# State-space and selection stages of a hybrid encoder step, rewritten on the vector engine: GELU without GpSimd, early weight remainders on DVE, a shorter threshold update and five-pass marks

## Chip, cores and metric

One core of one Trainium2 chip runs the kernel. The time is the device time of one execution in microseconds (us). Engines are named as in the profile: PE (TensorE), DVE (VectorE), ACT (ScalarE), POOL (GpSimd), SP (issues transfers).

## What is computed

One inference step of one layer, for 1024 prompt tokens and 32 sample tokens with 1024 channels:

```python
h = rms_norm(x, g_norm) * (1 + scale) + shift
z = h @ w_in                       # u, zs, q, k, v, za, qi, ki, wi, gates
hr, hi = scan(ab * h + bb @ u)     # S5: 32 groups, 64 complex states each
ys = gelu(c_re @ hr - c_im @ hi + d_skip * u)
ys = ys * sigmoid(ys @ w_glu + b_glu) * silu(zs)
score = sum_h(wi * relu(qi . ki))  # indexer; top 256 (sample: 136) keys
ya = softmax(q . k[selected]) @ v[selected] * silu(za)
out = (sigmoid(g_s) * (ys @ w_ps) + sigmoid(g_a) * (ya @ w_pa)) @ w_o
y = rms_norm(x + gate * out, g_final)
```

It also returns the keys, values, indexer keys and final states. All inputs and outputs are float32.

## The kernel before

**Precision.** A product of float32 matrices is made from three PE passes. Each weight tile is loaded raw, rounded to a high part (wh, by ACT, L46), and the remainder wl = raw - wh is taken by POOL (L49); PE then does wh x hH, wh x hL and wl x hH (L220 to L222). `ztile` (L626) does this for one tile of 128 output columns: 3 groups of tokens times 8 steps of depth times 3, so 72 matmuls of 128x352. Buffers for raw, wh and wl are two deep, so wh of tile n + 2 waits until PE has done tile n.

**Stages, in time.** From 0 to 66 us modulation, RMSNorm and the transposition of h, in an order written out by hand; DVE's state-space constants are held in a list and let go a few at a time. From 66 to about 112 us DVE works on the rest of these constants, while PE does u tiles and the first gate tiles. The constants include the powers TCt and TSt (128 of them for each of 16 state columns), doubled in seven steps (L415), each of which ends in `renorm`, six tiny DVE operations that bring the last power back to length 1.

From 110 to 250 us the state-space model runs in four quarters q = 0 to 3 of 8 groups. `build(q)` (L682) makes the matrices ER, EI (L698 to L700, DVE, each from two products in e2), G2 (L708 to L710), the skip term dm (L727) and the kernel Ksb (L734); PE transposes ER and EI (L723) and multiplies them. `chain_in` sends u through PE, `chain_scan` (L765) does rotation, scan and rotation back on DVE and leaves HS, `chain_out` (L803) multiplies with Tq (L811) and G2 (L812), copies the result to Yq (ACT, L813) and applies GELU on half quarters: Square on ACT (L817), two POOL operations (L818, L819), Tanh on ACT (L820), and one DVE operation (L821). Yq has one buffer; it is stored to DRAM as yD[q] when both halves are done. PE fills in with u and gate tiles. For q = 0 the G2 part of `build` runs on DVE, for the others on POOL.

GLU follows (257 to 315 us), which loads yD back, then the indexer's scores (315 to 445 us).

From 445 to 659 us come the selection and projections. The k-th largest score of each row is found bit by bit in 32 steps (`Grp.step`, L1162): in each, every row counts its scores at or above a trial threshold, on DVE for three score tiles (group A), on ACT for four (groups B1 and B2), and two or three tiny DVE operations set the bit. `mark` (L1194) then turns the threshold into a mask mb for each of the seven tiles: 1 for scores above it and for as many of the equal ones as are still needed, counted by a scan, as an addend of 0 or -BIG. PE meanwhile does the q, k, v and gate projections. The attention heads (L1052 scores into PSUM, L1053 adds the mask on DVE) begin when the masks stand.

Outside the part written by hand the order is set by the scheduler of the tile framework, which lays out each engine's instructions by a simulated timeline; each engine then takes its instructions strictly in that order.

Of the kernel before, what the change touches and what calls it, by code (L numbers as in the profile page):

```python
# [18 lines left out]
G3 = 352  # L19
KT = 8  # L20
EPS = 1e-6
BIG = 1e30
NCH = 133
NST = 134
QT = [(i * 128, 128, 128 * (i + 1)) for i in range(8)]
# [9 lines left out]
def body(nc, tc, I, O, dbg=None):  # L35
# [180 lines left out]
    def wsplit(src, kt, n, pool=None, heng=None, leng=None):  # L216
        return wparts(wload(src, kt, n, pool), kt, n, pool, heng, leng)
# [197 lines left out]
    for k in range(7):  # L415
        n = 1 << k
        cmul(TCt[:, :, n + 1:2 * n + 1], TSt[:, :, n + 1:2 * n + 1], TCt[:, :, 1:n + 1], TSt[:, :, 1:n + 1],
             bc(col(TCt, n), n), bc(col(TSt, n), n), n)
        renorm(2 * n)
    for t in (TCt, TSt):  # L420
        ve.tensor_copy(t[:, :, 129:134], t[:, :, 0:5])
    rho = tp_.tile([128, 16, 1], F32)
# [198 lines left out]
    stA.close()  # L621
    stQ.close()

    hz = [se]

    def ztile(c0, ncol, evac):  # L626
        wh, wl = wsplit(w_in[:, c0:c0 + ncol], KT, ncol, heng=hz[0])
        for n in range(3):
            ps = ps_z("pz")
            for k in range(KT):  # L630
                mm3(ps[:ncol, :G3], wh[:, k], wl[:, k], hH[n][:, k], hL[n][:, k], k == 0, k == KT - 1)
            evac(n, ps[:ncol, :G3])
# [49 lines left out]
    def build(q):  # L682
        Uq = xq.tile([128, 8, NCH], F32, name="Uq", bufs=2)
        sp.dma_start(Uq, uD[q].rearrange("(g m) s c -> (m s) g c", m=16))
        pr = slice(4 * q, 4 * q + 4)
        ER, EI = (xq.tile([128, 4, 16, 8], F32, name=n) for n in ("ER", "EI"))
        G2 = xq.tile([128, 8, 16, 8], F32, name="G2", bufs=2)
        e4 = [128, 4, 16, 8]

        def pw(t, lo):  # L690
            return t[:, pr, lo:lo + 8].unsqueeze(2).to_broadcast(e4)

        def bm(t):
            return t[:, pr].unsqueeze(3).to_broadcast(e4)

        def lin(eng, out, a, b, c, d, op):
            e2 = xq.tile(e4, F32, name="e2", tag="e2" + ("v" if eng is ve else "g"))
            eng.tensor_tensor(out, a, b, op=ALU.mult)  # L698
            eng.tensor_tensor(e2, c, d, op=ALU.mult)
            eng.tensor_tensor(out, out, e2, op=op)  # L700

        lin(ve, ER, pw(RR, 0), bm(BR), pw(RI, 0), bm(BI), ALU.subtract)
        lin(ve, EI, pw(RR, 0), bm(BI), pw(RI, 0), bm(BR), ALU.add)
        eng = ve if q == 0 else ge
        for e in range(2):
# [24 lines left out]
        for k in range(4):  # L730
            o = pt[:, 32 * k:32 * k + 32]
            te.matmul(o, fl(ER, k), CD[0][:, k], start=True, stop=False)
            te.matmul(o, fl(EI, k), CD[1][:, k], start=False, stop=True)
        ve.tensor_tensor(Ksb.rearrange("p g m -> p (g m)"), pt[:, 0:128], dm.rearrange("p g m -> p (g m)"), op=ALU.add)  # L734
        Tq = xq.tile([128, 8, 16, 8], F32, name="Tq", bufs=2)
        for hb in range(2):
            pT = ps_t()
            for s4 in range(4):
                te.matmul(pT[:, 128 * s4:128 * (s4 + 1)], shm[:, 4 * hb + s4], Ksb.rearrange("p g m -> p (g m)"),
                          start=True, stop=True)  # L740
            v = pT.rearrange("p (s g m) -> p g m s", s=4, m=16)
# [61 lines left out]
    def chain_out(q, ops, HS):  # L803
        Uq, G2, Bc, Tq = ops
        Yq = xq.tile([128, 8, NCH], F32, name="Yq")
        for g in range(8):
            k, r = g // 2, slice(64 * (g % 2), 64 * (g % 2) + 64)
            if g % 2 == 0:
                py = ps_s("py")
            o = py[:, 512 * (g % 2):512 * (g % 2) + NCH]  # L810
            te.matmul(o, Tq[:, g].rearrange("p m s -> p (m s)"), Uq[:, g], start=True, stop=False)  # L811
            te.matmul(o, G2[:, g].rearrange("p m s -> p (m s)"), HS[:, g % 2, g // 2, 0:NCH], start=False, stop=True)  # L812
            se.copy(Yq[:, g], o)  # L813
            if g % 4 == 3:
                yh = Yq[:, g - 3:g + 1]
                a1 = xq.tile([128, 4, NCH], F32, name="a1")
                se.activation(a1, yh, AF.Square)  # L817
                ge.tensor_scalar(a1, a1, 0.044715, 1.0, op0=ALU.mult, op1=ALU.add)  # L818
                ge.tensor_mul(a1, a1, yh)  # L819
                se.activation(a1, a1, AF.Tanh, scale=math.sqrt(2.0 / math.pi))  # L820
                ve.scalar_tensor_tensor(yh, a1, 1.0, yh, op0=ALU.add, op1=ALU.mult)  # L821
        sp.dma_start(yD[q].rearrange("(g m) s c -> (m s) g c", m=16), Yq)
# [322 lines left out]
    class Grp:  # L1145
# [16 lines left out]
        def step(self, b):  # L1162
# [11 lines left out]
                                 op0=ALU.bitwise_xor)  # L1174
                return
            x = self.thr
            if b or self.sign:
                ve.tensor_scalar(self.nxt, x, (1 << b - 1) if b else -(1 << 31), None, op0=ALU.bitwise_xor)
                x = self.nxt
            if self.sign:  # L1180
                ve.tensor_tensor(self.keep, self.cnt, self.lim, op=ALU.is_ge)  # L1181
            else:
                ve.tensor_tensor(self.keep, self.cnt, self.nse, op=ALU.is_lt)
            ve.scalar_tensor_tensor(self.thr, self.keep, b, x, op0=ALU.logical_shift_left, op1=ALU.bitwise_xor)

    A, B1, B2 = Grp(GA, "a", False), Grp(GB[:2], "b", True), Grp(GB[2:], "c", True)
    junk = sel.tile([128, 1024], BF16, tag="j", bufs=3, name="junk")
# [6 lines left out]
    def mark(g):  # L1194
        for k, m, nk, x in g.tiles():
            tk = g.thr.bitcast(F32)[:m, k:k + 1]
            cum = sel.tile([128, 1024], F32, name="cum")
            gt, eq = (sel.tile([128, 1024], BF16, name=n, tag="j", bufs=3) for n in ("gt", "eq"))
            ve.tensor_scalar(gt[:m, :nk], x[:m], tk, None, op0=ALU.is_gt, op1=ALU.add, accum_out=g.cnt[:m, k:k + 1])
            need = sel.tile([128, 1], F32, name="need", bufs=2)  # L1200
            ve.tensor_sub(need[:m], g.nse[:m, k:k + 1], g.cnt[:m, k:k + 1])
            ve.tensor_scalar(eq[:m, :nk], x[:m], tk, None, op0=ALU.is_equal)
            ve.tensor_tensor_scan(cum[:m, :nk], eq[:m, :nk], eq[:m, :nk], 0.0, op0=ALU.add, op1=ALU.max)
            ve.scalar_tensor_tensor(eq[:m, :nk], cum[:m, :nk], need[:m], eq[:m, :nk], op0=ALU.is_le, op1=ALU.mult)
            ve.tensor_tensor(gt[:m, :nk], gt[:m, :nk], eq[:m, :nk], op=ALU.max)
# [226 lines left out]
```

## Time and profile before

| | |
|---|---|
| median of 3 runs | 1135.89 us (1133.39 to 1137.15) |
| profiled execution | 1129.1 us, span 1127.3 us |
| mean granted PE clock | 0.961 |
| PE busy | 1026.3 us (91%), 6122 matmuls |
| DVE busy | 815.2 us (72%), 1922 instructions |
| ACT busy | 538.4 us (48%), 1129 instructions |
| POOL busy | 310.7 us (28%), 323 instructions |
| chain that ended last | PE 53%, DVE 28%, ACT 5%, issue 4%, DMA 3%, POOL 1% |

Busy shares are averages over stages with different limits. The chain follows the last instruction back to what released it; its shares tell on which engine the end was waiting, not how busy that engine was. In a waiting row, what stands behind the arrow is the instruction whose end released the waiting one.

### The profile page before, as it was taken

What the parts mean: (1) busy time and instruction counts of PE and PEld (TensorE: products, weight loads), DVE (VectorE), ACT (ScalarE), POOL (GpSimd) and SP (SyncE); (2) the same over time, 40 slices, a digit from 0 to 9 for tenths busy, and PEclk for the clock granted to TensorE, in tenths of its full rate; (3) what the DMA queues carried; (4) which work ended last, traced back from release to release, by engine and by line L of the source; (5) the groups of instructions that cost most, each with busy time, mean ns of one, the idle gap of its engine ahead of it and who ended that gap; (6) DMA issues with size and microseconds to landing.
All of it is one profiled execution on the core that took longest, in us unless ns stands there. A gap on an engine that the chain in (4) does not pass through costs nothing.

```text
span 1127.3 us, 17022 instructions
## 1 busy us (share of the span) xinstructions
PE 1026.3 (91%) x6122; PEld 943.5 (84%) x6122; DVE 815.2 (72%) x1922; ACT 538.4 (48%) x1129; POOL 310.7 (28%) x323
## 2 busy tenths in 40 slices
PE   6899898998999999978999969899996899999996
PEld 2689798998998899977899959789895699998774
DVE  5889999843435655999999975967748966687433
ACT  3541243435235545786786224655656665334111
POOL 2212535535030011232232202323227611220000
PEclk9989998999999999989999979999897999999998
DMA  9724213227331012231223322222333332854311
GB/s 357 191 76 116 76 39 78 77 89 230 124 98 47 19 57 89 84 90 53 76 96 96 124 59 57 66 87 57 95 91 110 114 113 86 232 167 144 126 62 51
DMA packets 115656, 115.50 MB, mean 102 GB/s; under 512 B 13372, under 2 KB 92688, under 8 KB 115572
## 3 DMA queue, kind: packets, MB, share of 16 engines
q1 hardware_dynamic: 115336, 114.36, 33.4%
q8 instruction: 48, 0.79, 0.3%
q14 instruction: 36, 0.29, 0.1%
q0 software_dynamic: 160, 0.03, 0.0%
q10 hardware_dynamic: 76, 0.02, 0.0%
HBM read 79.55 MB, written 30.08 MB: 97 GB/s over the span
## 4 chain that ended last, share of the span: by engine, by line
PE 53%; DVE 28%; ACT 5%; issue 4%; DMA 3%; POOL 1%; SPq 0%; DVEq 0%; POOLq 0%; ACTq 0%
PE pz L220 9%; PE pz L221 8%; PE pz L222 8%; DVE junk L1168 4%; PE pss L1052 3%; PE psm L1401 3%; PE psm L1403 3%; PE psm L1402 3%; PE pt L1108 2%; ACT junkb L1166 2%; PE pspo L1118 2%; PE pspo L1117 1%; PE pss L947 1%; PE pss L948 1%; PE psm L220 1%
## 5 line engine op out<-in xcount | busy, mean ns | idle before, releaser
L220 PE MATMUL pz<-hH,wh 128*128 128x352 f32 (+1 forms) x1080 | 361.7, 335 | 17.8 <-DVE zt L645 9.4
L221 PE MATMUL pz<-hL,wh 128*128 128x352 f32 (+1 forms) x1080 | 358.3, 332 | 0.7
L222 PE MATMUL pz<-hH,wl 128*128 128x352 f32 (+1 forms) x1080 | 356.9, 330 | 0.0
L49 POOL TENSOR_TENSOR wl<-raw,wh 128x1024 fp32r<-128x1024 f32 (+1 forms) x68 | 149.6, 2201 | 308.8 <-ACT wh L46 251.7
L220 PEld LDWEIGHTS pz<-hH,wh 128*128 128x128 f32 (+1 forms) x1080 | 208.2, 193 | 24.2 <-DVE zt L645 10.5
L221 PEld LDWEIGHTS pz<-hL,wh 128*128 128x128 f32 (+1 forms) x1080 | 207.8, 192 | 4.6 <-DVE hL L49 2.2
L222 PEld LDWEIGHTS pz<-hH,wl 128*128 128x128 f32 (+1 forms) x1080 | 207.6, 192 | 1.2
L1168 DVE TENSOR_SCALAR_CACHE_REDUCE junk<-sco,thra 128x1024 bf16<-128x1024 f32 (+2 forms) x96 | 96.8, 1009 | 0.3
L955 DVE SCALAR_TENSOR_TENSOR sco<-rl,wi,sco 128x384 f32<-128x384 f32 (+6 forms) x49 | 49.5, 1016 | 35.1 <-ACT rl L950 33.8
L46 ACT CAST wh<-raw 128x1024 fp32r<-128x1024 f32 (+2 forms) x53 | 46.5, 880 | 56.2 <-PE pz L221 36.6
L1053 DVE CUSTOM_DVE_ANT_0 Sm<-pss,mb 128x512 f32<-128x512 f32 (+4 forms) x68 | 39.8, 592 | 46.1 <-PE pt L1108 42.6
L1056 ACT ACTIVATE Sm<-Sm,mx 128x128 f32<-128x128 f32 (+8 forms) x68 | 52.9, 778 | 34.1 <-DVE mx L1053 33.6
L1110 ACT CAST PH<-pt 128x512 fp32r<-128x512 f32 (+2 forms) x96 | 44.4, 480 | 51.6 <-PE pspo L1117 26.1
L1166 ACT ACTIVATE junkb<-sco,thrb 128x896 bf16<-128x896 f32 x64 | 59.9, 936 | 17.9 <-DVE keepc L1181 6.4
L950 ACT ACTIVATE rl<-pss 128x384 f32<-128x384 f32 (+6 forms) x56 | 40.7, 737 | 48.8 <-PE pss L948 44.3
L1111 DVE TENSOR_TENSOR PL<-pt,PH 128x512 fp32r<-128x512 f32 (+2 forms) x96 | 51.5, 550 | 7.7 <-ACT PH L1110 5.9
L1403 PE MATMUL psm<-o,mL 128*128 128x512 f32 (+1 forms) x144 | 56.7, 395 | 0.0
L1401 PE MATMUL psm<-o,mH 128*128 128x512 f32 (+1 forms) x144 | 56.5, 394 | 0.0
L1402 PE MATMUL psm<-o,mH 128*128 128x512 f32 (+1 forms) x144 | 56.4, 394 | 0.0
L1052 PE MATMUL pss<-kH,qs 128*128 128x512 f32 (+2 forms) x96 | 38.0, 396 | 19.4 <-DVE mx L1053 17.7
L1108 PE MATMUL pt<-idf,Sm 128*128 128x128 f32 x288 | 46.9, 280 | 3.1 <-DVE PL L1111 2.7
L1118 PE MATMUL pspo<-PL,V 128*128 128x256 f32 x160 | 42.3, 295 | 6.3 <-DVE PL L1111 6.3
(402 smaller groups left out, 2175.2 us busy)
## 6 DMA issues: line engine op xcount, KB each, us to landing
raw<-in_w_in SPq DMA_DIRECT2D x44, 512.0 KB
thD<-tg SPq DMA_DIRECT2D x16, 528.0 KB
wm<-in_w_mod SPq DMA_DIRECT2D x8, 1024.0 KB
tgl<-thD SPq DMA_DIRECT2D x24, 176.0 KB
tgl<-thD SPq DMA_DIRECT2D x8, 528.0 KB
kd<-zf SPq DMA_DIRECT2D x32, 128.0 KB
raw<-in_w_mod SPq DMA_DIRECT2D x8, 512.0 KB
rawo<-in_w_o SPq DMA_DIRECT2D x8, 512.0 KB
```

The source lines that it names most:

```text
L49: leng.tensor_sub(l, src, f32(h))
L220: te.matmul(ps, wh, xh, start=first, stop=False)
L221: te.matmul(ps, wh, xl, start=False, stop=False)
L222: te.matmul(ps, wl, xh, start=False, stop=last)
L1052: te.matmul(S[:m, :w], lhsT, r[:, c], start=t == 0, stop=t == len(rhs) - 1)
L1108: te.transpose(pt[:, (k - b0) * 128:(k - b0 + 1) * 128], P[:, k * 128:(k + 1) * 128], idf)
L1118: te.matmul(po[:, 0:256], V2[:, k, e], PL[:, k], start=False, stop=k == nkt - 1)
L1166: se.activation(junkb[:m, :nk], x[:m], AF.Sign, bias=t, accum_out=self.cnt[:m, k:k + 1])
L1168: ve.tensor_scalar(junk[:m, :nk], x[:m], t, None, op0=ALU.is_ge, op1=ALU.add, accum_out=self.cnt[:m, k:k + 1])
L1401: te.matmul(ps, mh, wh, start=first, stop=False)
L1402: te.matmul(ps, mh, wl, start=False, stop=False)
L1403: te.matmul(ps, ml, wh, start=False, stop=last)
```

## The change

Seven edits:

1. BIG is 2^100 instead of 1e30.
2. `renorm` runs after doublings 1, 3 and 5 (odd k) only: four of seven calls fall away, 24 DVE operations of 128x16.
3. wl of the tiles u2, u3 and gates 0 to 5 is taken on DVE instead of POOL.
4. G2 is built on DVE for all quarters: 18 operations of 128x512 leave POOL.
5. GELU: the constant goes into Square's scale, so that one DVE scalar_tensor_tensor replaces the two POOL operations. This happens eight times.
6. The threshold update of group A takes two operations instead of three, in 30 of the steps.
7. Marks: le (at or below the threshold) and eq times BIG, the scan, and two scalar_tensor_tensor; the bf16 maximum (L1205) and the bf16 scaling (L1206) fall away.

```diff
-BIG = 1e30
+BIG = 2.0 ** 100
...
-        renorm(2 * n)
+        if k % 2:
+            renorm(2 * n)
...
-    hz = [se]
+    hz, lz = [se], [ve]
...
-        wh, wl = wsplit(w_in[:, c0:c0 + ncol], KT, ncol, heng=hz[0])
+        wh, wl = wsplit(w_in[:, c0:c0 + ncol], KT, ncol, heng=hz[0], leng=lz[0])
...
-        eng = ve if q == 0 else ge
+        eng = ve
...
-                se.activation(a1, yh, AF.Square)
-                ge.tensor_scalar(a1, a1, 0.044715, 1.0, op0=ALU.mult, op1=ALU.add)
-                ge.tensor_mul(a1, a1, yh)
+                se.activation(a1, yh, AF.Square, scale=math.sqrt(0.044715))
+                ve.scalar_tensor_tensor(a1, a1, 1.0, yh, op0=ALU.add, op1=ALU.mult)
...
     for f in range(NS):
         gate_tile(f)
+    lz[0] = ge
...
-            if b or self.sign:
-                ve.tensor_scalar(self.nxt, x, (1 << b - 1) if b else -(1 << 31), None, op0=ALU.bitwise_xor)
-                x = self.nxt
-            if self.sign:
-                ve.tensor_tensor(self.keep, self.cnt, self.lim, op=ALU.is_ge)
-            else:
-                ve.tensor_tensor(self.keep, self.cnt, self.nse, op=ALU.is_lt)
-            ve.scalar_tensor_tensor(self.thr, self.keep, b, x, op0=ALU.logical_shift_left, op1=ALU.bitwise_xor)
+            if not self.sign:
+                ve.tensor_scalar(self.keep, self.cnt, NSEL[self.ids[0]], float(1 << b), op0=ALU.is_lt, op1=ALU.mult)
+                ve.scalar_tensor_tensor(x, x, (1 << b - 1) if b else 0, self.keep, op0=ALU.bitwise_xor,
+                                        op1=ALU.bitwise_xor)
+                return
...
-            ve.tensor_scalar(gt[:m, :nk], x[:m], tk, None, op0=ALU.is_gt, op1=ALU.add, accum_out=g.cnt[:m, k:k + 1])
+            ve.tensor_scalar(le[:m, :nk], x[:m], tk, None, op0=ALU.is_le, op1=ALU.add, accum_out=g.cnt[:m, k:k + 1])
...
-            ve.tensor_sub(need[:m], g.nse[:m, k:k + 1], g.cnt[:m, k:k + 1])
-            ve.tensor_scalar(eq[:m, :nk], x[:m], tk, None, op0=ALU.is_equal)
+            ve.tensor_scalar(need[:m], g.cnt[:m, k:k + 1], NSEL[g.ids[k]] - nk, BIG, op0=ALU.add, op1=ALU.mult)
+            ve.tensor_scalar(eq[:m, :nk], x[:m], tk, BIG, op0=ALU.is_equal, op1=ALU.mult)
...
-            ve.tensor_tensor(gt[:m, :nk], gt[:m, :nk], eq[:m, :nk], op=ALU.max)
-            ve.tensor_scalar(mb[g.ids[k]][:m], gt[:m, :nk], 1.0, BIG, op0=ALU.subtract, op1=ALU.mult)
+            ve.scalar_tensor_tensor(mb[g.ids[k]][:m], le[:m, :nk], -BIG, eq[:m, :nk], op0=ALU.mult, op1=ALU.add)
```

From L419 on, line numbers of the changed kernel are one higher than those of the kernel before (up to the marks).

The scheduler lays the work out anew, on all engines. Three places of the order follow.

**First place: DVE in build(0).** ER is done with L700, now L701; PE waits for it with L723. Before:

```order
L698 TENSOR_TENSOR ER<-RR,BR 128x512
L699 TENSOR_TENSOR e_1065<-RI,BI 128x512
L698 TENSOR_TENSOR EI<-RR,BI 128x512
L727 TENSOR_TENSOR dm<-dsk,idf 128x128
L708 TENSOR_TENSOR G_1064<-P_1039,C_1041 128x4x128
L779 COPY rh<-rho 128x536
L781 MEMSET gr 128x4
L781 MEMSET gi 128x4
L708 TENSOR_TENSOR G_1064<-P_1039,C_1041 128x4x128
L700 TENSOR_TENSOR ER<-ER,e_1065 128x512
```

Now:

```order
L699 TENSOR_TENSOR EI<-RR,BI 128x512
L728 TENSOR_TENSOR dm<-dsk,idf 128x128
L709 TENSOR_TENSOR G_1040<-P_1015,C_1017 128x4x128
L780 COPY rh<-rho 128x536
L782 MEMSET gr 128x4
L782 MEMSET gi 128x4
L709 TENSOR_TENSOR G_1163<-P_1015,C_1017 128x4x128
L49 TENSOR_TENSOR wl<-raw,wh 128x1024
L709 TENSOR_TENSOR G_1040<-P_1015,C_1017 128x4x128
L709 TENSOR_TENSOR G_1163<-P_1015,C_1017 128x4x128
L701 TENSOR_TENSOR ER<-ER,e_1041 128x512
```

Ahead of ER's last operation stand two products of G2 for quarter 1 (G_1163) and a wl, the fifth of the eight; the other four stand further up, among the constants.

**Second place: GELU and G2.** In the kernel before POOL has both, here for the second half of quarter 0 (a_1307) and quarter 1 (G_1439):

```order
L708 TENSOR_TENSOR G_1439<-P_1039,C_1041 128x4x128 x2
L818 TENSOR_SCALAR a_1307<-a_1307 128x532
L710 TENSOR_TENSOR G_1439<-G_1439,e_1448 128x4x128
L819 TENSOR_TENSOR a_1307<-a_1307,Yq 128x532
L708 TENSOR_TENSOR e_1452<-P_1040,C_1042 128x512
L710 TENSOR_TENSOR G_1439<-G_1439,e_1452 128x4x128
```

Now DVE has GELU's operation (L819) between the scan of one quarter and the matrices of the next one but one, and a wl ahead of HS:

```order
L819 SCALAR_TENSOR_TENSOR a_1263<-a_1263,Yq 128x532
L699 TENSOR_TENSOR ER<-RR,BR 128x512
L784 MEMSET rh 128x4
L785 MEMSET rh 128x4
L735 TENSOR_TENSOR Ksb<-pt,dm 128x128
L699 TENSOR_TENSOR EI<-RR,BI 128x512
L821 SCALAR_TENSOR_TENSOR Yq<-a_1263,Yq 128x532
L728 TENSOR_TENSOR dm<-dsk,idf 128x128
L49 TENSOR_TENSOR wl<-raw,wh 128x1024
L793 TENSOR_TENSOR HS<-gr,gi 64x536
```

GELU's halves no longer pass through POOL's queue, and the scan's output HS stands behind a wl.

**Third place: PE at the end of the selection.** Before, the scores of the first heads (L1052) stand right behind the last transpositions:

```order
L1014 MATMUL pz<-idf,ckt 128x128 x4
L982 MATMUL pz<-idf,zf 128x128 x8
L982 MATMUL pz<-idf,zf 32x128
L1052 MATMUL pss<-kH_4470,qs_4472 128x512
L1052 MATMUL pss<-kL_4471,qs_4472 128x512
```

Now 19 matmuls of the next weight tile come between them; the first of them stand here:

```order
L1015 MATMUL pz<-idf,ckt 128x128 x4
L983 MATMUL pz<-idf,zf 128x128 x8
L983 MATMUL pz<-idf,zf 32x128
L220 MATMUL pz<-hH_80,wh 128x352
L221 MATMUL pz<-hL_83,wh 128x352
L222 MATMUL pz<-hH_80,wl 128x352
```

The scores of the heads, now L1053, follow on the nineteenth. Between the last y matmul (L812, now L813) and the first matmul of GLU the order of PE has 143 weight matmuls before and 134 now.

## Rows read from the trace of the kernel before

**Rows 1.** Busy us (count) by stretch and engine, PE clock, DMA share, GB/s.

```profile
110.00:250.00 140.00, 125.17 (x837) 122.89 (x836) 117.17 (x180) 53.10 (x127) 69.41 (x61) 0.95 0.27 77
250.00:262.00 12.00, 12.00 (x80) 12.00 (x79) 2.28 (x4) 4.07 (x8) 4.37 (x3) 1.00 0.37 94
...
445.00:656.00 211.00, 187.38 (x1126) 182.25 (x1125) 203.87 (x581) 141.70 (x321) 58.06 (x39) 0.95 0.30 89
```

**Rows 2.** Waits of PE, 110 to 250 us: total, times, longest.

```profile
PE pt L723 <- DVE rh L784: 5.4, 1, 5.4
PE pss L811 <- ACT Yq L813: 5.3, 3, 2.2
PE pt L739 <- DVE Ksb L734: 2.8, 1, 2.8
PE pt L723 <- DVE EI L700: 0.7, 1, 0.7
```

**Rows 3.** Timeline of POOL near 75 us: start, duration, instruction.

```profile
74.79 2.40 POOL L49 TENSOR_TENSOR wl<-raw,wh 128x1024 fp32r<-128x1024 f32 x1 [15.05 <-ACT wh L46]
```

**Rows 4.** Timeline of DVE at the same time.

```profile
74.71 0.19 DVE L268 TENSOR_TENSOR tB<-TSt 128x32 f32<-128x32 f32 x1
74.94 2.32 DVE L268 TENSOR_TENSOR TCt<-tA,tB 128x32 f32<-128x32 f32 x1
```

**Rows 5.** Groups of POOL instructions, shapes apart, 60 to 330 us.

```profile
L49 POOL TENSOR_TENSOR wl<-raw,wh 128x1024 fp32r<-128x1024 f32 x14 | 35.6, 2542 | 75.3 <-ACT wh L46 73.3 <-PE pt L739 2.0
L819 POOL TENSOR_TENSOR a<-a,Yq 128x532 f32<-128x532 f32 x8 | 12.4, 1548 | 0.5
L710 POOL TENSOR_TENSOR G<-G,e 128x512 f32<-128x512 f32 x6 | 10.3, 1715 | 0.2
L708 POOL TENSOR_TENSOR G<-P,C 128x512 f32<-128x512 f32 x6 | 7.9, 1327 | 12.2 <-DVE C L676 7.7 <-PE pss L812 4.5
L708 POOL TENSOR_TENSOR e<-P,C 128x512 f32<-128x512 f32 x6 | 7.6, 1275 | 0.3
L818 POOL TENSOR_SCALAR a<-a 128x532 f32<-128x532 f32 x8 | 6.4, 795 | 21.9 <-ACT a L817 21.7
```

**Rows 6.** Groups of DVE instructions, shapes apart, 66 to 260 us.

```profile
L710 DVE TENSOR_TENSOR G<-G,e 128x512 f32<-128x512 f32 x2 | 1.4, 692 | 0.1
...
L268 DVE TENSOR_TENSOR TCt<-tA,tB 128x1024 f32<-128x1024 f32 x1 | 1.2, 1225 | 0.0
```

**Rows 7.** Line 821 on DVE: min/median/max ns.

```profile
L821 DVE SCALAR_TENSOR_TENSOR Yq<-a,Yq x8: 705/714/1278, 170.4 to 256.1; 128x532 f32<-128x532 f32 x8
```

**Rows 8.** Timeline of DVE: first row of one renormalisation, first behind it.

```profile
88.08 0.18 DVE L268 TENSOR_TENSOR n<-TCt 128x16 f32<-128x16 f32 x1
...
89.06 0.69 DVE L268 TENSOR_TENSOR tA<-TCt 128x512 f32<-128x512 f32 x1
```

**Rows 9.** Chain that ended last, 203 to 221 us: start, duration, what.

```profile
202.94 3.11 POOL G L708 x2
...
214.37 5.89 DMA yD<-Yq
```

**Rows 10.** Timeline of DVE in one step of the bit search.

```profile
571.66 0.17 DVE L1178 TENSOR_SCALAR nxta<-thra 128x3 int32<-128x3 int32 x1
571.73 0.15 DVE L1181 TENSOR_TENSOR keepb<-cntb,limb 128x2 int32<-128x2 f32 x1
```

**Rows 11.** Timeline of DVE, marks of the widest tile.

```profile
616.27 1.28 DVE L1204 SCALAR_TENSOR_TENSOR eq<-cum,need,eq 128x1024 bf16<-128x1024 f32 x1
617.59 0.69 DVE L1205 TENSOR_TENSOR gt<-gt,eq 128x1024 bf16<-128x1024 bf16 x1
618.32 0.43 DVE L1206 TENSOR_SCALAR mb<-gt 128x1024 bf16<-128x1024 bf16 x1
618.66 0.61 DVE L1202 TENSOR_SCALAR eq<-sco,thra 128x768 bf16<-128x768 f32 x1
```

**Rows 12.** Wait of PE at the end of the selection.

```profile
PE pss L1052 <- DVE mx L1053: 11.3, 1, 11.3
```

More of the change, by code (lines that the diff above doesn't have):

```diff
@@ L1176, in step @@
             x = self.thr
-            if b or self.sign:
-                ve.tensor_scalar(self.nxt, x, (1 << b - 1) if b else -(1 << 31), None, op0=ALU.bitwise_xor)
-                x = self.nxt
-            if self.sign:
-                ve.tensor_tensor(self.keep, self.cnt, self.lim, op=ALU.is_ge)
-            else:
-                ve.tensor_tensor(self.keep, self.cnt, self.nse, op=ALU.is_lt)
-            ve.scalar_tensor_tensor(self.thr, self.keep, b, x, op0=ALU.logical_shift_left, op1=ALU.bitwise_xor)
+            if not self.sign:
[3 more added lines that the diff above has]
+                return
+            ve.tensor_scalar(self.nxt, x, (1 << b - 1) if b else -(1 << 31), None, op0=ALU.bitwise_xor)
+            ve.tensor_tensor(self.keep, self.cnt, self.lim, op=ALU.is_ge)
+            ve.scalar_tensor_tensor(x, self.keep, b, self.nxt, op0=ALU.logical_shift_left, op1=ALU.bitwise_xor)
     A, B1, B2 = Grp(GA, "a", False), Grp(GB[:2], "b", True), Grp(GB[2:], "c", True)
@@ L1197, in mark @@
             cum = sel.tile([128, 1024], F32, name="cum")
-            gt, eq = (sel.tile([128, 1024], BF16, name=n, tag="j", bufs=3) for n in ("gt", "eq"))
-            ve.tensor_scalar(gt[:m, :nk], x[:m], tk, None, op0=ALU.is_gt, op1=ALU.add, accum_out=g.cnt[:m, k:k + 1])
+            le, eq = (sel.tile([128, 1024], BF16, name=n, tag="j", bufs=3) for n in ("le", "eq"))
+            ve.tensor_scalar(le[:m, :nk], x[:m], tk, None, op0=ALU.is_le, op1=ALU.add, accum_out=g.cnt[:m, k:k + 1])
             need = sel.tile([128, 1], F32, name="need", bufs=2)
-            ve.tensor_sub(need[:m], g.nse[:m, k:k + 1], g.cnt[:m, k:k + 1])
-            ve.tensor_scalar(eq[:m, :nk], x[:m], tk, None, op0=ALU.is_equal)
+            ve.tensor_scalar(need[:m], g.cnt[:m, k:k + 1], NSEL[g.ids[k]] - nk, BIG, op0=ALU.add, op1=ALU.mult)
+            ve.tensor_scalar(eq[:m, :nk], x[:m], tk, BIG, op0=ALU.is_equal, op1=ALU.mult)
             ve.tensor_tensor_scan(cum[:m, :nk], eq[:m, :nk], eq[:m, :nk], 0.0, op0=ALU.add, op1=ALU.max)
             ve.scalar_tensor_tensor(eq[:m, :nk], cum[:m, :nk], need[:m], eq[:m, :nk], op0=ALU.is_le, op1=ALU.mult)
-            ve.tensor_tensor(gt[:m, :nk], gt[:m, :nk], eq[:m, :nk], op=ALU.max)
-            ve.tensor_scalar(mb[g.ids[k]][:m], gt[:m, :nk], 1.0, BIG, op0=ALU.subtract, op1=ALU.mult)
+            ve.scalar_tensor_tensor(mb[g.ids[k]][:m], le[:m, :nk], -BIG, eq[:m, :nk], op0=ALU.mult, op1=ALU.add)
     mark(A)
```

## Prediction

> **What bounds the kernel now.** I read the busy shares first (PE 91%, DVE 72%, ACT 48%, POOL 28%), then the busy time by stretch, PE's waits in each stretch, and last the timelines of DVE and POOL side by side. PE is the engine that is nearly always busy, so a change on DVE or POOL is worth only what PE waits for them, and what PE's clock loses around such waits. Two stretches hold almost all that this change can reach.
>
> In the state-space stretch, 110 to 250 us, PE is busy 125.2 of 140 us and its granted clock is 0.95 on average, a mixture of its two levels of 2.4 and 1.2 GHz [rows 1]. So 14.8 us are gaps, and the clock gives away another 0.05 x 140 = 7.0 us: 21.8 us is the ceiling. Of the gaps 5.4 us end with ER of build(0), which DVE finishes late, 2.8 us with Ksb, 0.7 us with EI (both DVE), and 5.3 us in three pieces with Yq [rows 2].
>
> In the selection, 445 to 656 us, DVE is busy 203.9 of 211 us [rows 1]: DVE is the bound there, PE fills in with projections. When these run out, PE waits 11.3 us until the last masks are ready [rows 12].
>
> **A DVE time that isn't DVE's work.** While POOL computes a wl, 2.40 us from 74.79 us [rows 3], a DVE addition of 128x32 that starts 0.15 us later takes 2.32 us; the same shape just before took 0.19 us [rows 4]. So one POOL wl costs DVE 2.13 us, although DVE could have done it in 1.23 us (an operation on two f32 tensors of 128x1024, [rows 6]). The three parts that leave POOL are of this kind: two f32 tensors in, one out.
>
> **The change, part by part.**
>
> *What POOL loses* [rows 5]: eight wl at 2.5 us (20.0), the 18 operations of G2 (10.3 + 7.9 + 7.6 = 25.8), the 16 of GELU (12.4 + 6.4 = 18.8); together 64.6 us. *What DVE gets*: eight wl at 1.23 (9.8), 18 operations at 0.69 (12.4) [rows 6], eight GELU operations priced as the other one of this form and shape, at its median of 0.71 (5.7) [rows 7]: 27.9 us. *What DVE loses*: four renormalisations of six tiny operations, 89.06 - 88.08 = 0.98 us each [rows 8], 3.9 us. Net work +24.0 us.
>
> *What DVE gets back from blocking.* From below nothing, if DVE's long operations had another cause; from above 64.6 us, if each moved POOL operation held DVE for all its time. I take two thirds, 43 us: the wl's price of 2.13 of 2.40 is near the upper end, but some G2 and GELU operations of POOL fall on DVE's idle 22.8 us of this stretch [rows 1] or beside each other. DVE then ends 43 - 24 = 19 us better off.
>
> *ER of build(0).* Ahead of it stand five of the eight wl (order, first place). Each is 2.13 - 1.23 = 0.9 us cheaper for DVE: 4.5 us. The renormalisations give 3.9. POOL's share of G2 beside this build (8.6 us of 25.8) blocked for two thirds, 5.7 us, and DVE now does two of its products, 1.4 us: 4.3. Against it stand up to 4 us in which DVE, in order, stands before a wl whose wh ACT hasn't written, because PE still uses the buffer. So ER comes 8.7 to 12.7 us sooner, and 5.4 is enough: this gap goes.
>
> *The rest of the stretch.* Ksb and EI, 3.5 us, come with DVE's relief. Of Yq's 5.3 us I take half, 2.6: the chain there runs through POOL's two G products of 3.11 us, then GELU on POOL, then the store of 5.89 us [rows 9], of which the change shortens all but the store; Yq has one buffer, so PE meets that store again when it comes sooner. Gaps gone: 5.4 + 3.5 + 2.6 = 11.5 us; clock in proportion, 7.0 x 11.5 / 14.8 = 5.4. I put back 4 us for two new waits, at places where the order leaves DVE only 0 to 2 us ahead of PE (Ksb and HS of later quarters, now behind a wl or G2). **Gain 13 us**, bounds 4 and 19.
>
> *GLU.* Between the last y matmul and the first GLU matmul, PE's order has 134 weight matmuls where it had 143. Nine at 0.15 us (80 in 12.00 us, [rows 1]) are 1.4 us less cover for the loads of y, whose time the change doesn't touch. **Cost 1.4 us**, bounds 4 lost and 2 gained.
>
> *Threshold update.* The removed nxta holds its place for 571.73 - 571.66 = 0.07 us only, though it takes 0.17 [rows 10]: the next one starts inside it. Thirty steps: 2.1 us, with 3.6 as the upper end if 0.12 us go.
>
> *Marks.* In the widest tile the two removed passes take 618.66 - 617.59 = 1.07 us; the one in their place has the form of L1204 but bf16 inputs alone. L1204 takes 617.59 - 616.27 = 1.32 us from start to start, the bf16 tensor_tensor 0.73 [rows 11]. The seven tiles (1024, 896, 768, 640, 544, 512 and 384 columns) have 4.66 times the widest one's, so the marks are between 1.2 us slower and 1.6 us faster. I take L1204, the same operation: 1.2 us slower. The other two replaced passes keep form and width. The Trainium skill, "VectorE: DVE Perf Modes", The perf-mode tier table, lists tensor_tensor in bf16 at 2x and tensor_scalar at 4x, and has no row for scalar_tensor_tensor; no run here shows that operation in bf16 alone. By that table's two entries the fusion is a loss, and the sum stays as it is; at 2x it would be 2.8 us better.
>
> *PE at the end of the selection.* 19 weight matmuls now stand ahead of the waiting L1053 (order, third place): 19 x 0.15 = 2.9 us of the 11.3 filled. With the masks 2.1 - 1.2 = 0.9 us sooner, **gain 3.8 us**, bounds 0.9 (if the weights aren't there) and 8.1 (2.9 + 3.6 + 1.6).
>
> BIG as a power of two changes no instruction's size. The Square's scale on ACT is an operand, priced at nothing because ACT is busy only 53.1 of 140 us here [rows 1]; if it cost, it would be on GELU's way to the store.
>
> **Sum.** 13.0 - 1.4 + 3.8 = 15.4 us off the profiled execution's 1129.1: 1113.7. That execution lies 6.8 us under the median of the runs, 1135.89, so I forecast 1120.5 us. The bounds of the terms, hardly all at one end together, give 1112 to 1130.
>
> **Rivals.**
>
> *DVE becomes the bound (slower).* DVE takes 24 us net of work into a stretch in which it idles 22.8 of 140 us. If its operations stay as long as they are (blocked by what POOL keeps, or by something else), ER comes later: five wl (6.1), two products (1.4), waits for wh (4), less 3.9 = 7.6 us; each later quarter adds 4.1 for G2 and 1.4 for GELU, 16.5 in all, of which DVE's idle hides two thirds or more. PE then loses 7.6 + 4.5 = 12 us, the selection returns 3.8: 1144 us. It decides where DVE's relief is under the 24 us it takes over. For it: DVE is busy 117.2 of 140 us there now, in PE's worst gaps nearly all the time. Against: the pair of rows 3 and 4. The Trainium skill, "Perfetto Trace Analysis", Optimizing Scalar/DVE Operations, speaks against this change: with DVE saturated it would offload to other engines, "or even GPSIMD"; but it adds that between those two this "might not help", since they share a port. By its first half this rival follows; the 2.13 us beside POOL's 2.40 side with the second. Chance 0.11.
>
> *The gaps move (no change).* ER, Ksb and Yq come sooner, PE runs into the store of 5.89 us, into wl behind DVE's queue and into GLU's loads, and the selection end gets back only what the marks lose. Then 11.5 us of gaps reappear as others, and the time stays within 3 us of 1136. For it: Yq's one buffer and the nine matmuls. Against: the largest gap, 5.4 us, has no such successor. Chance 0.12.
>
> *All of it (much faster).* All 21.8 us go, the marks run at 2x and the update gives 3.6: 21.8 + 8.1 - 1.4 = 28.5, or 1107 us. For it: the clock falls only around the gaps. Against: three Yq waits hang on a transfer that stays. Chance 0.13.
>
> **Numbers.** The forecast has 0.64. Range 1108 to 1134: it takes in the forecast's own 1112 to 1130, most of the largest gain and a part of no change; outside stay the slower case and the ends. A measurement of this kernel can tell about 0.3%, 3.4 us, from no change. Faster: 0.64 + 0.13 = 0.77; same 0.12; slower 0.11.
>
> **What would show it.** Right: the wait for ER gone, the clock at 1.0 in 110 to 250 us, PE's gaps there 4 to 7 us, DVE's 128x512 operations near 0.69 us, Yq waits of 2 to 3 us in all, 7 to 8 us for the masks, a bf16 mark near 1.28 us. Wrong: DVE above 95% in 110 to 250 us with PE's waits on it, wl standing before wh for long, or a new wait behind GLU's loads larger than 4 us.

## The result and the profile after

The changed kernel takes 1107.1 us (median of 4 runs, 1103.87 to 1108.77); the kernel before took 1134.64 us in its 4 runs by then. The ratio is 0.9756, interval 0.972 to 0.9792. Run again later beside other kernels, the change gave 1106.59 us and 0.978 (0.9739 to 0.9822). The forecast, 1120.5 us with a range of 1108 to 1134, had the sign right and the size too small: the time is 0.9 us below the range.

The profiled execution of the changed kernel takes 1107.44 us, with a span of 1105.7 us; the span before was 1127.3 us, so 21.6 us are gone. The same points of the program in both traces show where (us from the start of the span):

| | before | after | difference |
|---|---|---|---|
| last y matmul | 252.2 | 241.8 | -10.5 |
| first score matmul (after GLU) | 334.6 | 316.5 | -18.1 |
| first count of the bit search | 450.7 | 433.9 | -16.8 |
| last count | 609.1 | 591.1 | -18.1 |
| last mask | 658.9 | 642.1 | -16.8 |
| last matmul of the heads with the high part (L1117, now L1118) | 962.5 | 941.3 | -21.2 |
| last DVE operation | 1123.0 | 1101.3 | -21.7 |

PE's order differs, so that the weight matmuls that fill in stand at other places; the state-space stretch and GLU are therefore best read together: 18.1 us. Selection and heads together, from the first count on, give some 4 us in these two traces and 3 us in the second trace of each kernel. How that splits between the two stages is not steady: from the first count to the last mask it is 208.2 and 210.3 us before, 208.2 and 208.7 after. The busy times by stretch, cut at these points (columns as in [rows 1]), show the first part as a PE that hardly stands still:

```profile
80.00:242.00 162.00, 160.69 (x1102) 159.40 (x1101) 137.12 (x274) 61.95 (x146) 22.11 (x33) 1.00 0.32 94
...
434.00:642.00 208.00, 184.29 (x1111) 178.69 (x1109) 203.36 (x542) 137.10 (x312) 58.50 (x36) 0.96 0.28 84
```

In 80 to 242 us PE is busy 160.7 of 162 us at a granted clock of 1.00, the 2.4 GHz level throughout; the stretch of [rows 1] had 125.2 of 140 us at 0.95. PE's waits there, 105 to 241 us (total, times, longest), are down to two, where [rows 2] had 14.2 us in six:

```profile
PE pt L740 <- DVE rh L785: 0.8, 1, 0.8
PE pz L220 <- DVE zt L646: 0.4, 1, 0.4
```

DVE did not get less to do there, it got shorter operations. Groups of DVE's instructions before, shapes apart, 66 to 260 us (count, busy us and mean ns of one):

```profile
L727 DVE TENSOR_TENSOR dm<-dsk,idf 128x128 f32<-128x128 f32 x4 | 6.0, 1496 | 0.0
...
L774 DVE TENSOR_TENSOR gr<-w,w 128x532 f32<-128x532 f32 x4 | 4.9, 1220 | 0.1
...
L698 DVE TENSOR_TENSOR ER<-RR,BR 128x512 f32<-128x512 f32 x4 | 4.8, 1212 | 2.3 <-PE pt L732 2.3
```

The same operations after, 66 to 241 us, with what moved to DVE (L49, L711, L819):

```profile
L49 DVE TENSOR_TENSOR wl<-raw,wh 128x1024 fp32r<-128x1024 f32 x8 | 9.8, 1221 | 3.5 <-ACT wh L46 3.5
L819 DVE SCALAR_TENSOR_TENSOR a<-a,Yq 128x532 f32<-128x532 f32 x7 | 6.7, 956 | 2.2 <-ACT a L818 2.2
...
L711 DVE TENSOR_TENSOR G<-G,e 128x512 f32<-128x512 f32 x8 | 5.5, 686 | 0.2
...
L699 DVE TENSOR_TENSOR ER<-RR,BR 128x512 f32<-128x512 f32 x4 | 2.8, 707 | 3.0 <-PE pt L733 2.9
...
L775 DVE TENSOR_TENSOR gr<-w,w 128x532 f32<-128x532 f32 x4 | 2.8, 706 | 0.1
...
L728 DVE TENSOR_TENSOR dm<-dsk,idf 128x128 f32<-128x128 f32 x4 | 1.6, 402 | 0.0
```

dm fell from 1496 to 402 ns, gr from 1220 to 706, ER from 1212 to 707, without a change of shape. The moved operations cost what their shapes cost: 1221 ns for wl, 686 for G2; GELU's 956 is dearer than the 714 that I had taken.

In the selection PE still waits for the masks, 8.1 us instead of the 11.3 of [rows 12]:

```profile
PE pss L1053 <- DVE mx L1054: 8.1, 1, 8.1
```

And the timeline of DVE has the fused bf16 mark of the widest tile, and what starts behind it:

```profile
599.96 1.23 DVE L1206 SCALAR_TENSOR_TENSOR mb<-le,eq 128x1024 bf16<-128x1024 bf16 x1
601.22 0.62 DVE L1203 TENSOR_SCALAR eq<-sco,thra 128x768 bf16<-128x768 f32 x1
```

1.23 us, 1.26 from start to start: as long as if its inputs were f32, and longer than the 1.07 us of the two passes that it replaced [rows 11].

**PE's lost time.** For the experiments I use one measure, worked out from each trace: in a stretch, the time in which PE isn't busy, plus the stretch's length times one minus the granted clock. Idle + clock, us:

| kernel | 80 us to last y | last y to first score | first count to last mask | last mask to last head |
|---|---|---|---|---|
| before | 14.8 + 6.8 | 6.0 + 1.7 | 26.5 + 11.0 | 23.1 + 16.3 |
| before, profiled again | 16.4 + 6.8 | 6.1 + 1.7 | 27.1 + 13.7 | 24.2 + 11.9 |
| changed | 1.3 + 0 | 6.2 + 3.4 | 23.9 + 7.6 | 22.9 + 14.5 |
| changed, again | 2.0 + 0 | 7.1 + 1.7 | 23.4 + 9.2 | 23.3 + 14.7 |
| wl on POOL | 5.4 + 0 | 6.5 + 3.4 | 23.8 + 6.2 | 26.8 + 17.7 |
| G2 on POOL | 10.0 + 3.4 | 7.7 + 3.4 | 23.5 + 9.4 | 24.6 + 12.8 |
| GELU on POOL | 8.3 + 3.4 | 6.8 + 3.4 | 23.9 + 7.7 | 24.5 + 12.8 |
| all three on POOL | 18.7 + 11.9 | 4.9 + 1.7 | 23.4 + 9.3 | 24.7 + 12.8 |
| 24 idle products | 20.2 + 11.9 | 6.4 + 3.4 | 23.6 + 9.1 | 23.2 + 14.8 |
| 24 idle copies | 6.4 + 0 | 6.3 + 1.7 | 23.8 + 7.6 | 24.7 + 12.8 |
| old selection | 1.4 + 0 | 6.8 + 1.7 | 26.3 + 11.1 | 24.2 + 14.5 |
| every wl on DVE | 0 + 0 | 7.3 + 3.4 | 8.1 + 1.7 | 22.6 + 11.9 |
| before, every wl on DVE | 14.8 + 6.8 | 5.0 + 1.7 | 8.3 + 0 | 23.9 + 11.9 |
| no subtraction on POOL | 0 + 0 | 5.5 + 1.7 | 9.1 + 3.4 | 23.6 + 6.8 |

In this table the clock's part moves mostly in steps of some 1.7 us, so a difference of one step says little. The second measure is DVE's excess: over the DVE instructions from 66 to 235 us, each one's duration less the shortest of its operation and shape in that trace. It is 45 us before and 11 us in the changed kernel; with wl, G2 or GELU alone back on POOL it is 25, 22 and 19 us, and with all three 47 us.

### The profile page after: what moved, and what is told of

Same layout as the page of the kernel before. It is cut to its first block, busy times and chain, and to the rows that moved or that the text cites. A ratio compares the mean times of both kernels' runs of the same rounds, so it can differ in the third digit from the quotient of the medians.

```text
span 1105.7 us, 16957 instructions
## 1 busy us (share of the span) xinstructions
PE 1018.9 (92%) x6122; PEld 935.5 (85%) x6122; DVE 806.6 (73%) x1895; ACT 538.2 (49%) x1129; POOL 248.0 (22%) x281
## 4 chain that ended last, share of the span: by engine, by line
PE 63%; DVE 23%; ACT 6%; issue 4%; DMA 3%; POOL 0%; SPq 0%; DVEq 0%; POOLq 0%; ACTq 0%
PE pz L220 10%; PE pz L221 10%; PE pz L222 10%; DVE junk L1169 4%; ACT junkb L1167 3%; PE pss L1053 3%; PE psm L1401 3%; PE psm L1403 3%; PE psm L1402 3%; PE pt L1109 2%; PE pspo L1119 2%; PE pss L948 1%; PE pr L240 1%; PE pss L949 1%; PE pspo L1118 1%
## 5 line engine op out<-in xcount | busy, mean ns | idle before, releaser
L220 PEld LDWEIGHTS pz<-hH,wh 128*128 128x128 f32 (+1 forms) x1080 | 205.6, 190 | 27.2 <-DVE zt L646 12.3
L49 POOL TENSOR_TENSOR wl<-raw,wh 128x1024 fp32r<-128x1024 f32 (+2 forms) x60 | 132.1, 2203 | 311.3 <-ACT wh L46 261.3
L1053 PE MATMUL pss<-kH,qs 128*128 128x512 f32 (+2 forms) x96 | 37.7, 393 | 15.6 <-DVE mx L1054 13.9
L1384 ACT ACTIVATE tt<-xo 128x512 f32<-128x512 f32 (+1 forms) x18 | 11.4, 632 | 75.6 <-DVE xo L1382 46.6
```

The lines of the kernel that those rows point to most:

```text
L49: leng.tensor_sub(l, src, f32(h))
L220: te.matmul(ps, wh, xh, start=first, stop=False)
L1053: te.matmul(S[:m, :w], lhsT, r[:, c], start=t == 0, stop=t == len(rhs) - 1)
```

## The experiments

**The kernel before, again.** No edit.

> The kernel before, unchanged. Its first profiled execution (1129.1 us) was the shortest of its executions; the question is what the longer ones contain. If they lose more in 110 to 250 us, where the blocked DVE makes PE wait: a span of 1130 to 1135 us, with PE's gaps and clock loss there 24 to 28 us instead of 21.8. If the spread lies elsewhere (selection, heads): the same 21.8 us there and the rest behind 450 us. Time ratio 1.00 within 0.3%.

Measured: 1132.23 us, ratio 1.0002 (0.9976 to 1.0028); profiled execution 1128.9 us. Its waits between 80 us and the last y matmul are those of the first profile, 16.4 + 6.8 us. So both profiled executions lie under the medians of before (1130.1 to 1134.6 us in four groups of runs), and these two profiles don't show what the longer executions contain.

**One part back on POOL at a time.** Each edit on the changed kernel:

```diff
-    hz, lz = [se], [ve]
+    hz, lz = [se], [ge]
```

> The changed kernel with the eight wl back on POOL, all else as changed. Theory (a POOL operation on two f32 tensors holds DVE for nearly its whole time): DVE gains 8 x 1.23 = 9.8 us of work less and loses 8 x 2.13 = 17 us of blocking, 7 us net, five of the eight ahead of ER; the wait for ER comes back with 3 to 5 us and the time is 1110 to 1115 us. Rival (DVE's own work is what counts, blocking is hidden): DVE is relieved of 9.8 us, time 1102 to 1107 us.

Measured: 1120.3 us, ratio 0.9895 (0.986 to 0.993). In the state-space stretch PE idles 5.4 us instead of 1.3 to 2.0, as the blocking would have it, though in small pieces; the wait of 3 to 5 us for ER that I expected didn't come back:

```profile
PE pss L812 <- ACT Yq L814: 2.0, 2, 1.3
PE pt L477 <- DVE dl L475: 1.6, 1, 1.6
PE pt L724 <- DVE EI L701: 1.3, 1, 1.3
```

The time is 13.7 us longer, more than expected. Some 7 us of it lie in the heads, whose instructions the edit doesn't touch: 26.8 + 17.7 us lost there against 22.9 + 14.5. The scheduler has laid out all of the program anew. PE's waits in the heads for the masked scores (mx) grew from 16.5 us in 10 pieces to 23.3 in 17; why DVE is later there stays open.

```diff
-        eng = ve
+        eng = ve if q == 0 else ge
```

> The changed kernel with G2 of quarters 1 to 3 back on POOL. Theory of blocking: POOL's 25.8 us hold DVE for two thirds, 17 us, against 12.4 us of own work saved: DVE 5 us worse, PE's waits in 105 to 241 us rise from 1.2 us to 3 to 7 us, time 1109 to 1114 us. Rival (own work counts): time 1103 to 1107 us. If PE waits for G2 itself (POOL late) rather than for DVE, the row will name POOL.

Measured: 1122.26 us, ratio 0.9909 (0.9878 to 0.9941). The time is some 8 us above what I expected. PE's waits from 80 us to the last y matmul are on DVE but for 1.2 us, none on POOL, and larger than expected:

```profile
PE pt L724 <- DVE rh L785: 3.1, 1, 3.1
PE pss L812 <- DVE w L787: 3.0, 1, 3.0
PE pt L724 <- DVE stF L801: 2.7, 1, 2.7
PE pss L812 <- ACT Yq L814: 1.2, 1, 1.2
```

```diff
-                se.activation(a1, yh, AF.Square, scale=math.sqrt(0.044715))
-                ve.scalar_tensor_tensor(a1, a1, 1.0, yh, op0=ALU.add, op1=ALU.mult)
+                se.activation(a1, yh, AF.Square)
+                ge.tensor_scalar(a1, a1, 0.044715, 1.0, op0=ALU.mult, op1=ALU.add)
+                ge.tensor_mul(a1, a1, yh)
```

> The changed kernel with GELU's two operations back on POOL (16 operations, 18.8 us). Theory of blocking: DVE loses 12.5 us and saves 5.7, 7 us worse, spread as waits on DVE: 1110 to 1114 us. Rival (the chain through POOL to the store of y is what cost): the 5.3 us of waits on Yq come back, DVE's durations stay, 1110 to 1113 us; the waiting rows tell the two apart. Rival of no effect: 1107 us.

Measured: 1115.6 us, ratio 0.985 (0.9812 to 0.9889). The time is just above the ranges of both theories, and the waits name both causes, DVE (rh, ahead of Ksb) and Yq:

```profile
PE pt L740 <- DVE rh L785: 3.6, 1, 3.6
PE pss L812 <- ACT Yq L814: 2.8, 1, 2.8
```

So GELU's place on POOL cost through the blocking and through the store's chain.

**All three back on POOL.** The three edits together; the dropped renormalisations and the selection stay as changed.

> The changed kernel with wl, G2 and GELU all back on POOL; the dropped renormalisations, the threshold update and the marks stay. Undone alone the three cost 13, 15 and 9 us, 37 together, more than the whole gain of 24 to 28. Theory (each of the three alone already fills DVE's slack, the losses overlap): the state-space gain is gone, 1125 to 1131 us, ratio 0.993 to 1.000. Rival (the renormalisations, 3.9 us of DVE ahead of ER, carry a part of their own): 1115 to 1122 us.

Measured: 1132.03 us, ratio 0.9989 (0.9966 to 1.0011). The three large waits of before are back, at the same places as in [rows 2]:

```profile
PE pss L812 <- ACT Yq L814: 6.8, 3, 3.2
PE pt L724 <- DVE rh L785: 5.4, 1, 5.4
PE pt L740 <- DVE Ksb L735: 4.2, 1, 4.2
```

So without the three moves off POOL nothing is gained. But this isn't the kernel before again: the state-space stretch loses 18.7 + 11.9 us, 9.0 more than in the first trace of before (7.4 more than in the second), while selection and heads lose 70.2 us instead of 76.9, about as in the changed kernel. That the time equals that of before is in part such a cancellation; what makes the first stretch worse than before wasn't traced. The rival, a share that the renormalisations carry by themselves, doesn't show. Undone alone, the three cost 13.7, 15.7 and 9.0 us against the repeated run of the change, 38 together, for a whole of 25 (1131.5 less 1106.6): they are not additive.

**Work on POOL that nobody waits for.** On the changed kernel, in each of the eight GELU halves:

```diff
+                for _ in range(3):
+                    ge.tensor_mul(dm1, TCt[:, 0:4], TSt[:, 0:4])
```

dm1 is a scratch tile that nobody reads.

> The changed kernel with 24 idle products added on POOL in the state-space stretch (three per GELU half, two f32 tensors of 128x536 in, a scratch tile out that nobody reads). Nothing waits for them. Theory (a POOL operation of this kind holds DVE while it runs): 37 us of POOL work make DVE's operations there longer by 15 to 30 us in all, PE's waits on DVE come back and the time is 1113 to 1120 us. Rival (the old cost was the chain through POOL, or wl and G2 coming late from a slow engine): nobody waits, so 1105 to 1109 us.

Measured: 1132.15 us, ratio 1.0014 (0.9992 to 1.0035): the whole gain is gone, more than the theory's own range. By the traces PE, DVE, ACT and the rest of POOL's work have the same order of instructions as in the changed kernel (operation, shape and names; buffer numbers left out), so the products are the only difference. Half of them stand early, and one row of POOL's timeline holds eleven back to back:

```profile
103.40 15.81 POOL L823 TENSOR_TENSOR dm<-TCt,TSt 128x536 f32<-128x536 f32 x11
```

DVE's timeline at that time, behind it the first rows after POOL's last:

```profile
109.19 1.58 DVE L268 TENSOR_TENSOR tA<-br,sm 128x256 f32<-128x256 f32 x1
110.69 1.54 DVE L268 TENSOR_TENSOR tB<-bi,sm 128x256 f32<-128x256 f32 x1
112.26 1.42 DVE L268 TENSOR_TENSOR BR<-tA,tB 128x256 f32<-128x256 f32 x1
...
117.96 1.28 DVE L475 COPY dl<-dl 32x16 f32<-32x16 f32 x1
119.64 0.19 DVE L478 COPY dsk<-pt 128x32 f32<-128x32 f32 x1 [0.40 <-PE pt L477]
```

From 103.4 to 119.2 us operations of 128x256 take 1.4 to 1.6 us (0.42 to 0.43 in the last row of the copies below), and the copy of 32x16 takes 1.28 us; from 119.6 us they are short again. DVE gets about one operation in per product of POOL. PE pays (total, times, longest):

```profile
PE pt L742 <- DVE Ksb L737: 11.2, 1, 11.2
PE pt L477 <- DVE dl L475: 8.1, 1, 8.1
```

The wait on dl, 8.1 us, has nothing of POOL's in its chain: DVE alone is late. The one on Ksb isn't as clean, since PE needs POOL's small copies CD ahead of it and these queue among the products. So the time can hold more than blocking; the wait on dl and DVE's durations show blocking by itself. The excess of DVE from 66 to 235 us is 34 us, against 11 in the changed kernel: 23 us more for the 24 products' 36.5 us on POOL.

**The same with one input.** `ge.tensor_copy(dm1, TCt[:, 0:4])` in place of the product.

> As the run with 24 idle products on POOL, but with 24 idle copies (one f32 tensor of 128x536 in) that nobody reads. Theory A (any POOL access to memory holds DVE's two-tensor operations for its duration): copies of 0.7 to 1.0 us, 17 to 24 us in all, DVE's operations 10 to 20 us longer, time 1112 to 1125 us. Theory B (only POOL operations with two f32 tensors in do it): 1105 to 1109 us, DVE's durations as in the changed kernel.

Measured: 1110.69 us, ratio 0.9801 (0.9771 to 0.983). POOL's copies are shorter, and DVE's operations wait for them too. POOL, then DVE before and behind the last of the eight copies:

```profile
101.41 6.57 POOL L823 COPY dm<-TCt 128x536 f32<-128x536 f32 x8
```

```profile
106.63 0.86 DVE L268 TENSOR_TENSOR tA<-br,sm 128x256 f32<-128x256 f32 x1
107.41 0.84 DVE L268 TENSOR_TENSOR tB<-bi,sm 128x256 f32<-128x256 f32 x1
108.29 0.43 DVE L268 TENSOR_TENSOR BR<-tA,tB 128x256 f32<-128x256 f32 x1
```

Eight copies take 6.57 us. Two operations of 128x256 take 0.84 to 0.86 us beside them, and 0.43 us once they are over. The excess is 20 us. So a POOL copy holds DVE as well, for its shorter time. PE's order is again that of the changed kernel. The time lies between the two theories' ranges and its interval touches that of the change; the durations decide for theory A.

**Old threshold and old marks.** Both selection parts undone on the changed kernel.

> The changed kernel with the old threshold update and the old marks, both selection parts undone. Theory (30 times 0.07 us won, 1.2 us lost on the bf16 pass at 1.23 us): the masks come 0 to 2 us later than in the changed kernel, time within 3 us of it, 1104 to 1110 us. Rival (the selection edits carry a good part of the gain, as PE's loss fell by 6 us between first count and last mask): 1111 to 1114 us.

Measured: 1111.27 us, ratio 0.982 (0.9771 to 0.9869), against 0.978 for the change in the same group; the intervals of the ratios overlap, the times themselves (1110.2 to 1112.1 against 1105.0 to 1108.3) don't. From first to last count it is 158.2 us with the old update and 157.1 with the new one, from the last count to the last mask 49.8 us with the old marks and 51.1 with the new ones. Theory and trace agree on that: the masks come no sooner. But PE's last wait is back to its old length, because the scheduler has put the 19 weight matmuls behind it again:

```profile
PE pss L1053 <- DVE mx L1054: 11.3, 1, 11.3
```

The time is at the near edge of the rival's range. Of the 4.7 us that these parts gave, 3.2 are seen at this wait, as fill through PE's order and not through DVE's work.

**Every wl on DVE.** On the changed kernel:

```diff
-    lz[0] = ge
```

> The changed kernel with every wl of a projection tile on DVE, not the first eight alone. Theory of blocking: in the selection POOL does 15 wl of 2.57 us, each of which costs DVE about 2.1 us, where DVE needs 1.23 itself: DVE, the bound there, ends 13 us better off, the last mask comes 8 to 13 us sooner and the time is 1095 to 1102 us. Rival (order): a wl stands in DVE's queue until ACT has wh and PE frees a buffer, and the bit search stands behind it: masks later, 1108 to 1120 us.

Measured: 1085.42 us, ratio 0.9591 (0.9552 to 0.9631), 21 us under the changed kernel in the same group and 10 under my expectation. Busy times in the state-space stretch, the selection and the heads:

```profile
80.00:241.00 161.00, 161.00 (x1110) 160.65 (x1109) 133.13 (x277) 62.80 (x146) 10.74 (x29) 1.00 0.33 96
430.00:633.00 203.00, 194.89 (x1205) 191.11 (x1205) 195.19 (x561) 140.68 (x320) 20.89 (x23) 0.99 0.33 96
633.00:918.00 285.00, 262.41 (x1663) 236.94 (x1663) 207.55 (x546) 171.20 (x365) 81.39 (x110) 0.96 0.31 87
```

In the selection PE is busy 194.9 of 203 us at 0.99, and the long wait for the masks is gone. The last mask comes 202.3 us after the first count instead of 208.2, so DVE's saving there is 6 us, not 13, though it took over 15 wl; but PE does 1205 matmuls in the window instead of 1111, work that the heads no longer have to do: they last 285.2 us instead of 299.2.

**That edit alone, on the kernel before.** wsplit's `leng=ve` in `ztile`, nothing else.

> The kernel before with one edit alone: every wl of a projection tile on DVE. Theory of blocking: in the selection 13 us of DVE and in the state-space stretch 7 us come back; the 5.4 us wait for ER and the 11.3 us wait for the masks shrink to a few us: 1105 to 1115 us. Rival (order: DVE saturated by wl in the state-space stretch while G2 and GELU still block it): a gain in the selection only, 1115 to 1122 us.

Measured: 1105.13 us, ratio 0.9751 (0.9723 to 0.9779), as much as the whole change.

```profile
80.00:256.00 176.00, 161.21 (x1066) 158.09 (x1065) 142.00 (x267) 61.20 (x145) 57.90 (x61) 0.96 0.27 80
451.00:653.00 202.00, 193.73 (x1207) 189.94 (x1207) 195.75 (x594) 140.82 (x320) 21.26 (x22) 1.00 0.33 97
```

Here the rival's mechanism holds: the state-space stretch loses 21.6 us as before, and all of the gain is in the selection and behind it; that gain is larger than I had it for either theory, and that the time falls into the first theory's range is luck. DVE's excess in the state-space stretch falls from 45 to 26 us, and PE gains nothing by it: it still waits 5.5 us on Yq, 4.7 on Ksb and 3.3 for ER.

**No subtraction on POOL at all.** As every wl on DVE, with the remainders of keys, values, indexer keys, y and branch inputs and weights on DVE too (`leng=ve` at their splits).

> As the run with every projection wl on DVE, and also the remainders of keys, values, indexer keys, y of GLU and branch inputs and weights, so that POOL does no subtraction of two f32 tensors any more. Theory of blocking alone: each is cheaper on DVE than its blocking, 1075 to 1084 us. Rival: in the attention heads DVE stands on PE's path (PL, mx) and takes 25 to 30 us more in order ahead of them, while POOL's blocking there hits idle DVE time: 1086 to 1095 us.

Measured: 1095.25 us, ratio 0.9657 (0.9614 to 0.9699): 10 us worse than every wl on DVE, at the rival's far end. The two stand in different groups of runs; by their ratios it is 7 us, and the intervals overlap a little. In the heads:

```profile
637.00:928.00 291.00, 267.38 (x1693) 238.47 (x1692) 223.51 (x592) 171.34 (x367) 16.13 (x73) 0.98 0.30 88
```

DVE is busy 223.5 us there against 207.6, and the heads take 291.2 us against 285.2. But PE does 30 more matmuls in them, and by the measure of lost time they aren't worse: 23.6 + 6.8 us against 22.6 + 11.9. PE loses more behind them, up to the last DVE operation: 12.3 + 3.0 us against 5.5 + 0.3. That stretch here, with its longest wait, then in the kernel with every wl on DVE:

```profile
928.00:1090.00 162.00, 149.63 (x723) 125.05 (x721) 92.28 (x165) 41.05 (x88) 4.92 (x9) 0.98 0.39 125
PE psm L220 <- DVE m L1329: 4.0, 1, 4.0
```

```profile
918.00:1078.00 160.00, 154.60 (x769) 131.06 (x767) 94.59 (x162) 41.63 (x89) 16.83 (x17) 1.00 0.42 131
```

So the rival's time came, but its place, the heads, isn't borne out; which of the moved remainders costs wasn't isolated.

## Why the forecast was too small

The forecast was 1129.1 - 15.4 = 1113.7 us on the scale of the profiled execution, plus 6.8. The profile of the change has 1107.4 us. The miss of 13.4 us against the median is 6.3 us in the sum, 6.8 us in the scale, and 0.3 us that the change's profile lies over its own median. Two steps failed, the scale and the state-space term, about equally large; with either of them right, a range of this width would have held the time.

- **The scale.** The first step that failed is "That execution lies 6.8 us under the median of the runs": I carried it over to the changed kernel, which has no such distance, 1107.44 against 1107.1. In later groups of 13 to 16 runs the median of before is 1130.1 to 1134.2, so 1.7 to 5.8 us of the 6.8 came from having three runs.
- **Blocking: mechanism right, size too large.** POOL's operations hold DVE; the idle products show it with nothing else changed. I gave DVE back 43 us of 64.6; the excess fell by 34. That all three parts are "two f32 tensors in, one out" was misread: half of GELU's operations (L818 in [rows 5]) have one tensor in. It did no harm, since POOL's copies hold DVE too. The Trainium skill, "SBUF — State Buffer", SBUF: two separate sides, calls the pair of ports that DVE and GpSimd share an exclusive lock, held for a whole instruction. The 1.4 to 1.6 us of a 128x256 operation beside POOL agree with that, and so do DVE's copy of 32x16 and POOL's copies, which have one input.
- **State-space term: the second step that failed.** Gain 13, measured 21.6 - 1.3 = 20.3 us. "Gaps gone" went as forecast for ER, Ksb and EI. But the Yq waits went whole instead of half (2.7 us more) and the small gaps with them (0.6), the clock came back whole instead of "in proportion" (1.4), and the 4 us "put back" for new waits came out at 1.3 (2.7). Even the term's bound of 19 was passed. DVE ended better off by less than forecast and PE gained more: a PE wait is set by whether DVE is late at one place, not by the sum of DVE's work. Every wl on DVE in the kernel before shows the reverse, 19 us less excess and nothing for PE. "Hardly all at one end together" was wrong: the gaps, the clock and the new waits moved together. They don't all have one cause, though. The idle products, which block DVE but stand outside GELU's chain to the store, bring back 0.4 us of waits on Yq; GELU alone on POOL brings back 2.8 and all three parts 6.8, so the Yq gaps belong to that chain as well. How much of the 20.3 us is blocking and how much is the chain isn't shown.
- **GLU.** Cost 1.4, measured 9.6 - 7.7 = 1.9 us of lost time, 1.0 in the second traces: right, though this is no more than a step of the clock.
- **Threshold and marks.** 2.1 won and 1.2 lost; measured 158.4 - 157.1 = 1.3 (160.5 - 157.6 = 2.9 in the second traces) and 51.1 - 49.8 = 1.3. The choice of L1204's rate for the bf16 mark was right: 1.23 us, the tensor_tensor in bf16 took 0.69. The Trainium skill, "VectorE: DVE Perf Modes", The perf-mode tier table, lists no rate for this form; the run gives that of one f32 pass.
- **End of the selection.** Gain 3.8, measured 3.2 at the wait for the masks; from first score to the end the two traces differ by 3.6. Right.
- **The rivals.** "All of it" (1107) came out in the state-space stretch, 20.3 of its 21.8 us, but not with the marks at 2x and 3.6 us from the update. Its number fits by luck: it takes 28.5 us off the first median, and between the two traces 21.7 are gone. "The gaps move" didn't happen: 1.3 us of gaps are left. "DVE becomes the bound" fell with DVE's relief: DVE is busy 137.1 of 162 us. A wl costs DVE 1.22 us if DVE does it, and cost it 2.13 us of waiting while POOL did it [rows 3 and 4]. The Trainium skill, "Perfetto Trace Analysis", Optimizing Scalar/DVE Operations, says that offloading between DVE and GpSimd "might not help", and these numbers agree.

## What to carry to other kernels

When POOL computes on tensors while DVE is busy, price its operation as DVE time for up to as long as POOL takes (2.13 of 2.40 us for one wl, 23 of 36.5 us for the idle products), and compare it with the time that DVE itself would need; in a stage that DVE bounds, 2.5 us on POOL against 1.2 on DVE decides for DVE. Where DVE isn't the bound, test each move: taking the last subtractions off POOL cost 7 to 10 us here. When one change removes several late arrivals at PE, take their gaps and the clock around them together, and don't carry a profile's distance to a median of three runs over to another kernel.

## What was not expected

- One edit in place of seven does as much: every wl of the projections on DVE, 1105.1 us on the kernel before, and 1085.4 us on the changed one, the best version here.
- POOL copies with one input hold DVE's two-tensor operations too (0.84 to 0.86 us instead of 0.43).
- Edits that change no work at a place move its order: PE's wait for the masks went from 8.1 to 11.3 us with the selection's old code, through 19 matmuls, though the masks came at the same distance from the first count (207.9 us against 208.2).
- In the selection DVE's saving by wl was 6 us, but the whole gain 21: PE's filling work moved from the heads into the selection, where it ran beside DVE.
